# Output projection: the two halves of a token tile split to f16 in SBUF and turned by DMA instead of by TensorE

## The chip, the cores and the metric

The kernel runs on one core of a Trainium2 chip. The metric is the device time of one execution in microseconds (us), as the median of several runs.

## What is computed

One encoder layer over 4096 tokens plus 16 learned meta tokens, width 1024. A combined input projection feeds a Fourier branch (512 wide) and a grouped-query attention branch (8 query heads, 2 key/value heads of 64), both gated. Their outputs, side by side, go through one output projection, a residual add and a final RMSNorm:

```
u = rmsnorm(h, norm_g); proj = u @ w_in
f_out = fourier_branch(f_in) * silu(f_gate)            # 512 channels
a_out = attention_branch(q, k, v) * silu(a_gate)       # 512 channels
mixed = concat([f_out, a_out])                         # 1024 channels
h = h + mixed @ w_out
out = rmsnorm(h, final_g)[16:]
```

All inputs are float32. The kernel carries values as a sum of two f16 parts (a high part and what is left), so a product takes three matmuls: high x high, high x low, low x high.

## The kernel before

**Two phases.** `phase_a` does the input projection, the folding and the first half of the Fourier branch, and writes its results to DRAM. `phase_b` is attention. The Fourier branch's rest is dealt out among attention's first block; its result `f_out` lands in DRAM as `mf_d` (4096 x 512 f32). The order on every engine is the order in which the code is written; nothing reorders it.

**Pairs and steps.** `phase_b` runs over 32 pairs `i = 4b + p`: 8 blocks `b` of 512 queries, 4 pairs `p` of heads. A pair has 66 steps `j` (two heads, 33 key tiles each). Step `j`:

- `qk` (two matmuls of 512 columns, lines 1100 and 1101, into a PSUM tile `s`, of which there are two), then ACT's exp `pe` (line 1104), then the f16 rest `rr` (line 1106), on GpSimd (POOL) or, at the steps in `on_dve`, on VectorE;
- `pvm`, the product with the values (lines 1121 to 1128), of the step five before: `LAG = 5`. It reads `pe` and `rr`.

At the 16 steps in `AT` two score groups of the next pair are multiplied (line 1031, PSUM tile `m`, of which there are two) and reduced by VectorE (line 1033) to a row maximum.

**Output projection of the block before.** While pair `(b, p)` runs, the token tile `s = p` (128 tokens) of block `b-1` is projected. Steps of a pair that matter here: `TR = 12` (turn the tile), `O0 = 15` and `O1 = 39` (first matmul of the first and of the second half of the output columns; one matmul of 24 per step, line 1181, tile `po`), `NORM` (the final norm of the tile before). In a half, matmuls 0 to 11 read the Fourier channels and 12 to 23 the attention channels. So attention's part is first read at step 27.

Matmuls want the channels on the partitions, so the tile must be turned. `out_tr` does it at step 12: eight f32 transposes on TensorE (line 1164; four from `mf`, the Fourier half loaded from `mf_d`, four from `obs`, attention's output in SBUF) into one `m` tile, ACT's copy to the f16 high parts `mh` (line 1167) and at step 13 VectorE's subtraction to the low parts `ml` (line 1169).

**The tail.** The last block's four tiles are projected after attention's end. `tail_tr(s, part)` transposes four blocks into an `s` tile (line 1346; part 0 Fourier, part 1 attention), ACT writes the high parts (line 1349) and VectorE the low ones (line 1350) into `hv` and `lv`, which are the idle query buffers `qA` and `qB`; `tail_mm` multiplies (line 1361), `tail_end` normalises and stores.

**Queues.** Nearly all DMAs of `phase_b` are issued by SyncE (SP), which waits in order: gates `ag` (`gload`, line 802), queries of the next block (`qload`, lines 780 to 785; line 780 is a transposing DMA from DRAM), `mf` (line 1147), the residual `xr` (line 1152), the result `out` (line 1214).

Of the kernel before, what the change touches and what calls it, by code (L numbers as in the profile page):

```python
# [22 lines left out]
F32 = mybir.dt.float32  # L23
F16 = mybir.dt.float16
BF16 = mybir.dt.bfloat16
I32 = mybir.dt.int32
AF = mybir.ActivationFunctionType
ALU = mybir.AluOpType
# [4 lines left out]
P = 128  # L33
D = 1024
# [12 lines left out]
WS = 64.0  # L47
# [3 lines left out]
NQB = NTOK // QB  # L51
# [688 lines left out]
def phase_b(tc, a, pool, mm3, id32, id16, sc):  # L740
# [5 lines left out]
    V, S, T, G = nc.vector, nc.scalar, nc.tensor, nc.gpsimd  # L746
    dma, dma_t = nc.sync.dma_start, nc.sync.dma_start_transpose
    q_d, k_d, v_d, fg_d, ag_d, mf_d, wo_d, ld = (
        sc[n] for n in ("q_d", "k_d", "v_d", "fg_d", "ag_d", "mf_d", "wo_d", "ld"))
    LAG = 5  # L750
    with ExitStack() as st:
        bp = pool(st, "bp")
        w1 = pool(st, "b1", 1)
        w2 = pool(st, "b2", 2)
        wk = pool(st, "bw", LAG + 3)
        sm = pool(st, "bs", 2)
        pm = pool(st, "pm", 2, PSUM)
# [5 lines left out]
        qA = [bp.tile([P, NH, QB], F16, name=f"qA{i}") for i in range(2)]  # L763
        qB = [bp.tile([P, NH, QB], F16, name=f"qB{i}") for i in range(2)]
# [39 lines left out]


        wvh, wvl = ld["wv"]
        bias, stk8 = (w2.tile([P, 512], F32, tag="mf", name=n) for n in ("bias", "stk8"))
        stk = w1.tile([P, 4, P], F32, tag="hh", name="stk")
        thl = w1.tile([P, 2, 2, 4, P], F16, tag="yo", name="thl")
        mos = w2.tile([P, 4, 512], F32, tag="ob", name="mo")  # L810
# [329 lines left out]

            return qk, pvm

        pst = {}

        def load_mf(b, s):
            mf = w2.tile([P, 512], F32, tag="mf", name="mf")
            dma(mf, mf_d[b * QB + s * P:b * QB + s * P + P])
            pst[b, s] = [mf, None]

        def load_xr(b, s):  # L1150
            xr = pst[b, s][-1] = w2.tile([P, D], F32, tag="xr", name="xr")
            dma(xr, a["x"][b * QB + s * P:b * QB + s * P + P])

        def out_load(b, s):
            load_mf(b, s)
            load_xr(b, s)

        def out_tr(b, s):
            mf, xr = pst[b, s]
            t = pm.tile([P, 2, 512], F32, tag="m", name="m")  # L1160
            tv = t.rearrange("p a (b c)->p (a b) c", c=P)
            for j in range(8):
                src = mf[:, j * P:(j + 1) * P] if j < 4 else obs[b][:, s, (j - 4) * P:(j - 3) * P]
                T.transpose(tv[:, j], src, id32)  # L1164
            mh = ld["sh1"].tile([P, 8, P], F16, tag="mh", name="mh")
            ml = ld["sh1"].tile([P, 8, P], F16, tag="ml", name="ml")
            S.activation(mh, tv, AF.Copy)
            pst[b, s] = [mh, ml, xr]
            return lambda: V.tensor_tensor(out=ml, in0=tv, in1=mh, op=ALU.subtract)

        def out_units(b, s):

            d = {}

            def one(k, j):
                mh, ml, xr = pst[b, s]
                if j == 0:
                    d["po"] = pp.tile([P, 512], F32, tag="po", name="po")
                cs = slice(k * 512, (k + 1) * 512)
                i, w = j // 3, j % 3  # L1180
                T.matmul(d["po"], (ml if w == 2 else mh)[:, i],  # L1181
                         wol[i // 4][:, i % 4, cs] if w == 1 else woh[0][:, i, cs], start=j == 0, stop=j == 23)
                if j == 23:
                    if k == 0:
                        d["hh"] = w1.tile([P, D], F32, tag="hh", name="hh")
                    V.scalar_tensor_tensor(out=d["hh"][:, cs], in0=d["po"], scalar=1.0 / WS, in1=xr[:, cs],  # L1186
                                           op0=ALU.mult, op1=ALU.add)

            return [[(lambda k=k, j=j: one(k, j)) for j in range(24)] for k in range(2)], d

        def out_end(b, s, d):

            xr, hh = pst.pop((b, s))[-1], d["hh"]
            ss = sm.tile([P, 1], F32, tag="ss", name="ss")
            rf = sm.tile([P, 1], F32, tag="rf", name="rf")

            def square():
                S.activation(xr, hh, AF.Square, accum_out=ss)

            t = sm.tile([P, 1], F32, tag="r1t", name="r1t")  # L1200
            h = sm.tile([P, 1], F32, tag="r1h", name="r1h")

            def guess():
                V.tensor_scalar(out=ss, in0=ss, scalar1=1.0 / D, scalar2=EPS, op0=ALU.mult, op1=ALU.add)
                root0(rf, ss, t, h)

            def newton():
                root1(rf, t, h)

            def scale():  # L1210
                yo = w1.tile([P, D], F32, tag="yo", name="yo")
                V.scalar_tensor_tensor(out=yo, in0=hh, scalar=rf, in1=fgb[0], op0=ALU.mult, op1=ALU.mult)
                t0 = b * QB + s * P
                dma(a["out"][t0:t0 + P], yo)

            return square, guess, newton, newton, newton, scale
# [51 lines left out]
        def block0(g, mid):  # L1268
# [8 lines left out]
            if not flist and not fgb:  # L1277
# [3 lines left out]
                wo_load()  # L1281
                release()

        pend = []
        prev = None
        for i, (b, p) in enumerate(pairs):
            if p == 1 and b + 1 < NQB:
                qload(b + 1)
            if i > 4:
                out_load(b - 1, p)  # L1290
            elif i == 4:
                load_mf(0, 0)
            gs, last = [], {}
            if i + 1 < len(pairs):
                gs, meta, red, fin, put = max_units(i + 1)
                last = {61: red, 63: fin, 64: put}
                if meta:
                    last[MT] = meta[0]
            halves = None
            on_dve = {j + 2 for j in AT[:-1]} | {2 * NT + 1}  # L1300
            if i + 1 == len(pairs):
                on_dve = {j for j in range(2 * NT + 2) if j % 3}
            for j, (qk, pvm) in enumerate(stream(i)):
                qk(V if j in on_dve else G)
                if halves:
                    for k, o in ((0, O0), (1, O1)):
                        if o <= j < o + 24:
                            halves[0][k][j - o]()
                n = 2 if j in AT else 0
                if j == TR and b > 0:  # L1310
                    low = out_tr(b - 1, p)
                    halves = out_units(b - 1, p)
                for f in gs[:n]:
                    f()
                gs = gs[n:]
                if j in last:
                    last[j]()
                if i < 5:
                    block0(66 * i + j, j - 2 in AT)
                if i == 4 and j == 28:  # L1320
                    load_xr(0, 0)
                if j == LAG + 2 and i + 1 < len(pairs):
                    gload(i + 1)
                if j == 20 and i + 1 == len(pairs):
                    load_mf(b, 0)
                    load_mf(b, 1)
                    load_xr(b, 0)
                if j == TR + 1 and b > 0:
                    low()
                if j in NORM and prev:  # L1330
                    prev[NORM.index(j)]()
                if j == 62 and b > 0:
                    prev = out_end(b - 1, p, halves[1])
                pend.append(pvm)
                if len(pend) > LAG:
                    pend.pop(0)()


        b = NQB - 1
        hv, lv = (t[(b + 1) % 2].rearrange("p h (a c)->p (h a) c", c=P) for t in (qA, qB))  # L1340

        def tail_tr(s, part):
            src = pst[b, s][0] if part == 0 else obs[b][:, s]
            t = pq.tile([P, 512], F32, tag="s", name="s")
            for j in range(4):
                T.transpose(t[:, j * P:(j + 1) * P], src[:, j * P:(j + 1) * P], id32)
            x = slice(4 * (2 * s + part), 4 * (2 * s + part) + 4)
            tv = t.rearrange("p (j c)->p j c", c=P)
            S.activation(hv[:, x], tv, AF.Copy)
            V.tensor_tensor(out=lv[:, x], in0=tv, in1=hv[:, x], op=ALU.subtract)  # L1350
# [12 lines left out]
                                 start=i == 0 and w == 0, stop=i == 7 and w == 2, skip_group_check=True)  # L1363

        def tail_end(s):
            acc, xr = accs.pop(s), pst.pop((b, s))[1]
            yo = w1.tile([P, D], F32, tag="yo" if s % 2 else "hh", name="yo")
            ss = sm.tile([P, 2], F32, tag="ss2", name="ss2")
            rf = sm.tile([P, 1], F32, tag="rf", name="rf")
# [16 lines left out]
            t0 = b * QB + s * P  # L1386
            dma(a["out"][t0:t0 + P], yo)

        tail_tr(0, 0)
        tail_tr(1, 0)  # L1390
        prev[0]()
        while pend:
            pend.pop(0)()
# [2 lines left out]
        for f in prev[1:]:  # L1396
            f()
        load_xr(b, 1)
        tail_tr(0, 1)
        tail_tr(1, 1)  # L1400
        load_mf(b, 2)
        load_mf(b, 3)
        tail_mm(0, 1)
        tail_end(0)
        tail_tr(2, 0)
        tail_tr(2, 1)
        tail_mm(1, 1)
        tail_end(1)
        load_xr(b, 2)
        load_xr(b, 3)  # L1410
        tail_tr(3, 0)
        tail_tr(3, 1)
        tail_mm(2, 0)
        tail_mm(2, 1)
        tail_end(2)
# [138 lines left out]
```

## Time and profile before

| | |
|---|---|
| median of 3 runs | 3228.03 us (3224.39 to 3229.53) |
| the profiled execution | 3225.34 us, of which the span is 3223.6 us |
| busy: TensorE (PE), VectorE (DVE), ACT, POOL | 3169.3, 2366.2, 1671.4, 2270.3 us |
| granted TensorE clock | 0.995 |
| step 12 of pair 4, the first turned tile | 1123 us after the span's start |
| end of attention, start of the tail | about 3165 us |

Times in the profile are from the span's start. A row of a timeline has the start, the duration, the engine and what ran; `[0.19 <-PE s L1101]` at its end is how long the engine had been idle and what ended that. A row of the chain of waits has the start, the share of the end-to-end chain that the piece holds, and the piece. PE's matmuls overlap, so their duration is longer than their distance; the chain gives the distance.

### The profile page before, as it was taken

How to read it: one execution, taken by the hardware profiler on the slowest of the kernel's cores; microseconds unless marked ns; L12 is line 12 of the kernel's file. 1: busy time of each engine (PE TensorE's matmuls, PEld its weight loads, DVE VectorE, ACT ScalarE, POOL GpSimd, SP SyncE). 2: the span in 40 equal slices, each digit the busy share in tenths (PEclk: the TensorE clock that was granted, in tenths of full speed). 3: DMA queues.
4: the chain of work that ended last, by engine and by line, in shares of the span. 5: the costliest groups of instructions: out<-in, count | busy, mean ns of one | idle time of the engine just before them, and what ended most of it. 6: DMA issues, size and time to landing. Idle time of an engine off the chain costs nothing.

```text
span 3223.6 us, 77420 instructions
## 1 busy us (share of the span) xinstructions
PE 3169.3 (98%) x32531; PEld 1858.7 (58%) x32531; DVE 2366.2 (73%) x3213; ACT 1671.4 (52%) x2937; POOL 2270.3 (70%) x2174
## 2 busy tenths in 40 slices
PE   8999999998999999999999999999999999999998
PEld 4555555545666655555555555555555555555564
DVE  6666566647677777777787777778777877777764
ACT  5433333324555555555555555555555555555553
POOL 4655565537777777777777777777777777777762
PEclk9999999999999999999999999999999999999999
DMA  7444545548422300011001000100110010000011
GB/s 237 149 160 149 156 147 167 176 160 219 130 62 82 102 26 21 21 40 45 21 21 47 21 24 21 47 21 27 36 42 21 21 47 21 25 21 22 21 37 60
DMA packets 175344, 231.95 MB, mean 72 GB/s; under 512 B 71170, under 2 KB 119170, under 8 KB 172050
## 3 DMA queue, kind: packets, MB, share of 16 engines
q1 hardware_dynamic: 161170, 201.83, 20.5%
q10 hardware_dynamic: 13824, 25.17, 2.1%
q8 instruction: 254, 4.16, 0.5%
q14 instruction: 96, 0.79, 0.1%
HBM read 139.59 MB, written 66.38 MB: 64 GB/s over the span
## 4 chain that ended last, share of the span: by engine, by line
PE 74%; DVE 1%; issue 1%; ACT 0%; DMA 0%; POOL 0%; SPq 0%; ACTq 0%; DVEq 0%
PE s L1101 14%; PE s L1100 14%; PE o L1121 13%; PE po L1181 9%; PE m L1031 8%; PE o L1128 8%; PE o L1126 2%; PE o L1124 2%; PE pd L848 2%; PE m L1361 1%; PE m L1164 1%; DMA acs<-acs_d 0%; ACT pe L1104 0%; DVE thl L892 0%; DVE mx L1033 0%
## 5 line engine op out<-in xcount | busy, mean ns | idle before, releaser
L1106 POOL TENSOR_TENSOR rr<-pe 128x512 f16<-128x512 f32 x1572 | 1680.7, 1085 | 522.3 <-ACT pe L1104 516.3
L1104 ACT ACTIVATE pe<-s 128x512 f32<-128x512 f32 x2112 | 1260.7, 597 | 1030.3 <-PE s L1101 882.6
L1033 DVE TENSOR_REDUCE mx<-m 128x2 f32<-128x1024 f32 x1024 | 1206.3, 1220 | 181.8 <-PE m L1031 176.7
L1128 PE MATMUL o<-VV,rr 128*128 128x65 f16 x8448 | 975.5, 193 | 0.0
L1128 PEld LDWEIGHTS <-rr 128*128 128x128 f16 x8448 | 785.3, 98 | 168.3 <-POOL rr L1106 1.3
L1121 PE MATMUL o<-VV,pe 128*128 128x129 f16 x6336 | 840.5, 222 | 0.4 <-ACT tt L1132 0.4
L1101 PE MATMUL s<-qB,K 128*128 128x512 f16 x2112 | 800.8, 379 | 1.4 <-DVE qB L1068 1.4
L1100 PE MATMUL s<-qA,K 128*128 128x512 f16 x2112 | 800.0, 379 | 0.5 <-ACT pe L1104 0.5
L1121 PEld LDWEIGHTS <-pe 128*128 128x128 bf16 x6336 | 590.8, 97 | 361.7 <-issue 190.8
L1106 DVE TENSOR_TENSOR rr<-pe 128x512 f16<-128x512 f32 x540 | 450.7, 835 | 228.6 <-ACT pe L1104 224.4
L1124 PE MATMUL o<-VV,pe 128*128 128x65 f16 x2112 | 411.5, 195 | 0.0
L1126 PE MATMUL o<-VV,pe 128*128 128x64 f16 x2112 | 410.6, 194 | 0.0
L303 PE MATMUL ps<-wh,xh 128*128 128x512 f16 (+2 forms) x1032 | 353.7, 354 | 9.6 <-ACT xh L291 9.6
L304 PE MATMUL ps<-wl,xh 128*128 128x512 f16 (+2 forms) x1032 | 353.6, 354 | 2.3 <-DVE wl L274 2.3
L1031 PE MATMUL m<-K,qP 64*128 64x512 f16 x2048 | 314.1, 383 | 9.5 <-DMA qP<-qA 5.9
L306 PE MATMUL ps<-wh,xl 128*128 128x512 f16 x768 | 291.6, 380 | 0.0
L1126 PEld LDWEIGHTS <-pe 128*128 128x128 bf16 x2112 | 209.2, 99 | 0.0
L1124 PEld LDWEIGHTS <-pe 128*128 128x128 bf16 x2112 | 206.6, 98 | 0.0
L1101 PEld LDWEIGHTS <-K 128*128 128x128 f16 x2112 | 205.2, 97 | 1.6 <-issue 1.6
L1100 PEld LDWEIGHTS <-K 128*128 128x128 f16 x2112 | 203.6, 96 | 1.6 <-issue 1.4
L1031 PEld LDWEIGHTS <-qP 64*128 64x128 f16 x2048 | 59.8, 94 | 229.4 <-issue 221.5
L1181 PE MATMUL po<-woh,mh 128*128 128x512 f16 x448 | 169.8, 379 | 0.9 <-DVE hh L1186 0.9
(207 smaller groups left out, 3468.0 us busy)
## 6 DMA issues: line engine op xcount, KB each, us to landing
room<-x SPq DMA_DIRECT2D x32, 512.0 KB
xt<-xt SPq DMA_DIRECT2D x32, 512.0 KB
sg<-fx SPq DMA_DIRECT2D x16, 1024.0 KB
xr<-x SPq DMA_DIRECT2D x32, 512.0 KB
out<-yo SPq DMA_DIRECT2D x32, 512.0 KB
ct<-cdo SPq DMA_DIRECT2D x9, 1088.0 KB
fg_d<-g ACTq DMA_DIRECT2D x32, 256.0 KB
ag_d<-g ACTq DMA_DIRECT2D x32, 256.0 KB
```

The lines of the kernel that those rows point to most:

```text
L303: T.matmul(o, xh[:, d, :n], wh[:, d, c0:c1], start=d == 0, stop=False)
L1031: T.matmul(t[:, e], q[rs, p, s * P:(s + 1) * P], K[kv][rs, 0, c * 512:(c + 1) * 512], start=True, stop=True)
L1033: V.tensor_reduce(mx[:, s, :, c], t, axis=AX.X, op=ALU.max)
L1100: T.matmul(s, K[kv][:, 0, t * P:(t + 1) * P], qa, start=True, stop=False)
L1101: T.matmul(s, K[kv][:, 1, t * P:(t + 1) * P], qb, start=False, stop=True)
L1104: S.activation(pe, s, AF.Exp, scale=HD ** -0.5)
L1106: eng.tensor_tensor(out=rr, in0=pe, in1=hi, op=ALU.subtract)
L1121: T.matmul(o[:, c0:c0 + 129], hi[:, cs], va, start=t == 0 and s == 0, stop=t == NT, skip_group_check=True)
L1124: T.matmul(o[:, c0:c0 + 65], hi[:, cs], vh, start=False, stop=t == NT, skip_group_check=True)
L1126: T.matmul(o[:, c0:c0 + 64], hi[:, cs], vl, start=False, stop=t == NT, skip_group_check=True)
L1128: T.matmul(o[:, c0:c0 + 65], rr[:, cs], vh, start=False, stop=t == NT, skip_group_check=True)
L1181: T.matmul(d["po"], (ml if w == 2 else mh)[:, i], wol[i // 4][:, i % 4, cs] if w == 1 else woh[0][:, i, cs], start=j == 0, stop=j == 23)
```

## The change

The TensorE transposes of the output projection are replaced in the steady part, and for the Fourier half in the tail too. A half of a token tile (128 tokens x 512 channels, f32 in SBUF) is copied to f16 high parts by ACT and its low parts are subtracted by VectorE, both from SBUF to SBUF, side by side in one tile of 128 x 1024 f16. A transposing DMA from SBUF to SBUF turns the eight 128 x 128 blocks of it.

- Fourier half: `load_mf` at step 40 of the pair before, ACT at step 50, VectorE at 51, the DMA to `mt` at 53. For the first tile, in pair 4, the load stands at the pair's start and the steps are 6, 7 and 8.
- Attention half: ACT at step 12, VectorE and the DMA to `at` at step 13.
- Last pair: four Fourier tiles, loaded at steps 20, 31, 42, 53; ACT, VectorE and two DMAs (high parts to `hv`, low parts to `lv`) from steps 26, 37, 48 and 59.
- Tiles: `mf` shares a buffer with the new `ah` (tag `ml`), `hl` takes the tag `mh`, `mt` and `at` are new, one buffer each. The Fourier branch's `bias` and `stk8` share one buffer of tag `xr`.
- The tail transposes only attention's four blocks of each tile.

```diff
-        bias, stk8 = (w2.tile([P, 512], F32, tag="mf", name=n) for n in ("bias", "stk8"))
+        bs = w2.tile([P, 2, 512], F32, tag="xr", name="bs")
+        bias, stk8 = bs[:, 0], bs[:, 1]
...
         def load_mf(b, s):
-            mf = w2.tile([P, 512], F32, tag="mf", name="mf")
+            mf = mfs[b, s] = ld["sh1"].tile([P, 512], F32, tag="ml", name="mf")
             dma(mf, mf_d[b * QB + s * P:b * QB + s * P + P])
...
+        def mf_parts(b, s):
+            mf = mfs.pop((b, s))
+            hl = ld["sh1"].tile([P, 2, 512], F16, tag="mh", name="hl")
+            def high():
+                S.activation(hl[:, 0], mf, AF.Copy)
+            def low():
+                V.tensor_tensor(out=hl[:, 1], in0=mf, in1=hl[:, 0], op=ALU.subtract)
+            def turn():
+                mt = w1.tile([P, 8, P], F16, tag="mt", name="mt")
+                dma_t(mt, hl.rearrange("p w c->p (w c)"))
+                mts[b, s] = [mt]
+            def turn_last():
+                dma_t(hv[:, 8 * s:8 * s + 4], hl[:, 0])
+                dma_t(lv[:, 8 * s:8 * s + 4], hl[:, 1])
+            return high, low, turn_last if b + 1 == NQB else turn
...
         def out_tr(b, s):
-            mf, xr = pst[b, s]
-            t = pm.tile([P, 2, 512], F32, tag="m", name="m")
-            tv = t.rearrange("p a (b c)->p (a b) c", c=P)
-            for j in range(8):
-                src = mf[:, j * P:(j + 1) * P] if j < 4 else obs[b][:, s, (j - 4) * P:(j - 3) * P]
-                T.transpose(tv[:, j], src, id32)
-            mh = ld["sh1"].tile([P, 8, P], F16, tag="mh", name="mh")
-            ml = ld["sh1"].tile([P, 8, P], F16, tag="ml", name="ml")
-            S.activation(mh, tv, AF.Copy)
-            pst[b, s] = [mh, ml, xr]
-            return lambda: V.tensor_tensor(out=ml, in0=tv, in1=mh, op=ALU.subtract)
+            src = obs[b][:, s]
+            hl = ld["sh1"].tile([P, 2, 512], F16, tag="ml", name="ah")
+            S.activation(hl[:, 0], src, AF.Copy)
+            def low():
+                V.tensor_tensor(out=hl[:, 1], in0=src, in1=hl[:, 0], op=ALU.subtract)
+                at = w1.tile([P, 8, P], F16, tag="at", name="at")
+                dma_t(at, hl.rearrange("p w c->p (w c)"))
+                mts[b, s].append(at)
+            return low
...
-                T.matmul(d["po"], (ml if w == 2 else mh)[:, i],
+                T.matmul(d["po"], mts[b, s][i // 4][:, i % 4 + (4 if w == 2 else 0)],
...
+                if i == 4 and j == 6:
+                    ready = dict(zip((6, 7, 8), mf_parts(0, 0)))
+                if i + 1 == len(pairs):
+                    if 20 <= j < 60 and j % 11 == 9:
+                        load_mf(b, j // 11 - 1)
+                    if j >= 26 and j % 11 == 4:
+                        ready = dict(zip((j, j + 1, j + 2), mf_parts(b, j // 11 - 2)))
+                elif i >= 4:
+                    if j == 40:
+                        load_mf(*divmod(i - 3, 4))
+                    if j == 50:
+                        ready = dict(zip((50, 51, 53), mf_parts(*divmod(i - 3, 4))))
+                if j in ready:
+                    ready[j]()
...
-        tail_tr(0, 0)
-        tail_tr(1, 0)
         prev[0]()
...
-        tail_tr(2, 0)
-        tail_tr(2, 1)
+        tail_tr(2)
         tail_mm(1, 1)
         tail_end(1)
...
-        tail_tr(3, 0)
-        tail_tr(3, 1)
+        tail_tr(3)
```

**On TensorE** at step 12 of a steady pair, between the scores (lines 1100, 1101) and the product with the values (from line 1121), before:

```order
L1101 LDWEIGHTS K_7267
L1101 MATMUL s<-qB_7272,K_7267 128x512
L1164 MATMUL m<-id_72,mf 128x128 x4
L1164 MATMUL m<-id_72,ob 128x128 x4
L1121 LDWEIGHTS pe
L1121 MATMUL o<-VV,pe 128x129
```

The two rows of line 1164 stand there no more; the product with the values follows the scores directly, as at any other step. The matmuls of the output projection stay where they were and read `mt` and `at`.

**On ACT**, one pair from the end of one head to step 12, before (`tt` is the end of a head, `xr,ss` the square of the norm at step 9, `mh` step 12):

```order
L1132 ACTIVATE tt<-o 128x452
L1104 ACTIVATE pe<-s 128x512 x33
L1132 ACTIVATE tt<-o 128x452
L1104 ACTIVATE pe<-s 128x512 x5
L1198 ACTIVATE xr,ss<-hh 128x1024
L1104 ACTIVATE pe<-s 128x512 x3
L1167 ACTIVATE mh<-m 128x1024
```

and now (line numbers after the edit: 1105 is the exp, 1133 the end of a head, 1214 the square):

```order
L1133 ACTIVATE tt<-o 128x452
L1105 ACTIVATE pe<-s 128x512 x13
L1155 ACTIVATE hl<-mf 128x512
L1105 ACTIVATE pe<-s 128x512 x20
L1133 ACTIVATE tt<-o 128x452
L1105 ACTIVATE pe<-s 128x512 x5
L1214 ACTIVATE xr,ss<-hh 128x1024
L1105 ACTIVATE pe<-s 128x512 x3
L1178 ACTIVATE ah<-ob 128x512
```

One copy of 1024 elements out of PSUM at step 12 became two of 512 out of SBUF, one at step 50 of the pair before and one at step 12. VectorE's subtraction is split in the same way, to steps 51 and 13.

**On SP**, a pair in which the next block's queries are loaded, before:

```order
L1214 DMA out<-yo 128x1024
L780 DMA_TRANSPOSE qA_7269<-q_d 128x4x512 x2
L783 DMA qP_7273<-qA_7269 64x2x512 x4
L785 DMA qB_7271<-qA_7269 64x2048 x2
L1147 DMA mf<-mf_d 128x512
L1152 DMA xr<-x 128x1024
L802 DMA ag<-ag_d 128x4x128
L1214 DMA out<-yo 128x1024
```

and now (1230 is the result's store, 1148 the load of `mf`, 1173 the residual's):

```order
L1230 DMA out<-yo 128x1024
L1148 DMA mf<-mf_d 128x512
L1162 DMA_TRANSPOSE mt<-hl 128x8x128
L780 DMA_TRANSPOSE qA_7269<-q_d 128x4x512 x2
L783 DMA qP_7273<-qA_7269 64x2x512 x4
L785 DMA qB_7271<-qA_7269 64x2048 x2
L1173 DMA xr<-x 128x1024
L802 DMA ag<-ag_d 128x4x128
L1183 DMA_TRANSPOSE at<-ah 128x8x128
L1230 DMA out<-yo 128x1024
```

The `mt` DMA, which waits for VectorE's step 51, now stands ahead of the next pair's query loads and residual, and the `at` DMA between the gates and the store. In the whole program SP issues 64 more transposing DMAs: 28 to `mt`, 28 to `at`, 8 in the last pair.

More of the change, by code (lines that the diff above doesn't have):

```diff
@@ L1141, in step @@
             return qk, pvm
-        pst = {}
+        pst, mts, mfs = {}, {}, {}
         def load_mf(b, s):
-            mf = w2.tile([P, 512], F32, tag="mf", name="mf")
+            mf = mfs[b, s] = ld["sh1"].tile([P, 512], F32, tag="ml", name="mf")
             dma(mf, mf_d[b * QB + s * P:b * QB + s * P + P])
-            pst[b, s] = [mf, None]
+        def mf_parts(b, s):
[13 more added lines that the diff above has]
+            return high, low, turn_last if b + 1 == NQB else turn
@@ L1150, in load_xr @@
         def load_xr(b, s):
-            xr = pst[b, s][-1] = w2.tile([P, D], F32, tag="xr", name="xr")
+            xr = pst[b, s] = w2.tile([P, D], F32, tag="xr", name="xr")
             dma(xr, a["x"][b * QB + s * P:b * QB + s * P + P])
-        def out_load(b, s):
-            load_mf(b, s)
-            load_xr(b, s)
         def out_tr(b, s):
-            mf, xr = pst[b, s]
-            t = pm.tile([P, 2, 512], F32, tag="m", name="m")
-            tv = t.rearrange("p a (b c)->p (a b) c", c=P)
-            for j in range(8):
-                src = mf[:, j * P:(j + 1) * P] if j < 4 else obs[b][:, s, (j - 4) * P:(j - 3) * P]
-                T.transpose(tv[:, j], src, id32)
-            mh = ld["sh1"].tile([P, 8, P], F16, tag="mh", name="mh")
-            ml = ld["sh1"].tile([P, 8, P], F16, tag="ml", name="ml")
-            S.activation(mh, tv, AF.Copy)
-            pst[b, s] = [mh, ml, xr]
-            return lambda: V.tensor_tensor(out=ml, in0=tv, in1=mh, op=ALU.subtract)
+            src = obs[b][:, s]
@@ L1175, in one @@
             def one(k, j):
-                mh, ml, xr = pst[b, s]
                 if j == 0:
@@ L1185, in one @@
                         d["hh"] = w1.tile([P, D], F32, tag="hh", name="hh")
-                    V.scalar_tensor_tensor(out=d["hh"][:, cs], in0=d["po"], scalar=1.0 / WS, in1=xr[:, cs],
+                    V.scalar_tensor_tensor(out=d["hh"][:, cs], in0=d["po"], scalar=1.0 / WS, in1=pst[b, s][:, cs],
                                            op0=ALU.mult, op1=ALU.add)
@@ L1191, in out_end @@
         def out_end(b, s, d):
-            xr, hh = pst.pop((b, s))[-1], d["hh"]
+            xr, hh = pst.pop((b, s)), d["hh"]
             ss = sm.tile([P, 1], F32, tag="ss", name="ss")
@@ L1282, in block0 @@
                 release()
+        hv, lv = (t[NQB % 2].rearrange("p h (a c)->p (h a) c", c=P) for t in (qA, qB))
         pend = []
@@ L1289, in phase_b @@
             if i > 4:
-                out_load(b - 1, p)
+                load_xr(b - 1, p)
             elif i == 4:
                 load_mf(0, 0)
+            ready = {}
             gs, last = [], {}
@@ L1324, in phase_b @@
                 if j == 20 and i + 1 == len(pairs):
-                    load_mf(b, 0)
-                    load_mf(b, 1)
                     load_xr(b, 0)
@@ L1339, in phase_b, with tail_tr @@
         b = NQB - 1
-        hv, lv = (t[(b + 1) % 2].rearrange("p h (a c)->p (h a) c", c=P) for t in (qA, qB))
-        def tail_tr(s, part):
-            src = pst[b, s][0] if part == 0 else obs[b][:, s]
+        def tail_tr(s):
+            src = obs[b][:, s]
             t = pq.tile([P, 512], F32, tag="s", name="s")
@@ L1346, in tail_tr @@
                 T.transpose(t[:, j * P:(j + 1) * P], src[:, j * P:(j + 1) * P], id32)
-            x = slice(4 * (2 * s + part), 4 * (2 * s + part) + 4)
+            x = slice(8 * s + 4, 8 * s + 8)
             tv = t.rearrange("p (j c)->p j c", c=P)
@@ L1365, in tail_end @@
         def tail_end(s):
-            acc, xr = accs.pop(s), pst.pop((b, s))[1]
+            acc, xr = accs.pop(s), pst.pop((b, s))
             yo = w1.tile([P, D], F32, tag="yo" if s % 2 else "hh", name="yo")
@@ L1398, in phase_b @@
         load_xr(b, 1)
[L1399 to L1402, printed above, removed]
+        tail_tr(0)
+        tail_tr(1)
         tail_mm(0, 1)
         tail_end(0)
-        tail_tr(2, 0)
-        tail_tr(2, 1)
+        tail_tr(2)
         tail_mm(1, 1)
```

## The prediction

> **What bounds the kernel now.** I read the page's busy shares first, then the chain of waits, then the pair that holds a turned tile.
>
> ```profile
> span 3223.6 us, 77420 instructions
> PE 3169.3 (98%) x32531; PEld 1858.7 (58%) x32531; DVE 2366.2 (73%) x3213; ACT 1671.4 (52%) x2937; POOL 2270.3 (70%) x2174
> L1101 PE MATMUL s<-qB,K 128*128 128x512 f16 x2112 | 800.8, 379 | 1.4 <-DVE qB L1068 1.4
> L1100 PE MATMUL s<-qA,K 128*128 128x512 f16 x2112 | 800.0, 379 | 0.5 <-ACT pe L1104 0.5
> L1128 PEld LDWEIGHTS <-rr 128*128 128x128 f16 x8448 | 785.3, 98 | 168.3 <-POOL rr L1106 1.3
> ```
>
> PE is busy 98% of the span, and that alone proves little, since its matmuls overlap. The last columns say more: before the 4224 score matmuls PE stood idle 1.9 us in all, and its weight load waited 1.3 us for `rr`. So in attention nothing holds PE up, and what PE no longer does comes off the end, as long as nothing else becomes late. The chain around the turned tile of one pair shows what that is:
>
> ```profile
> 2669.23 0.22 PE s L1100
> 2669.45 0.22 PE s L1101
> 2669.67 0.06 PE o L1121
> ...
> 2670.23 0.22 PE s L1101
> 2670.45 0.87 PE m L1164 x8
> 2671.32 0.06 PE o L1121
> ```
>
> Step 11 goes from the scores straight to the product with the values; step 12 has 0.87 us of transposes between, on the chain and without a gap on either side.
>
> **Term 1: the steady transposes leave PE.** One such group per tile; ACT's copy that follows each counts the tiles:
>
> ```profile
> L1167 ACT ACTIVATE mh<-m 128x1024 f16<-128x1024 f32 x28 | 28.6, 1023 | 6.1 <-PE m L1164 6.1
> L1169 DVE TENSOR_TENSOR ml<-m,mh 128x1024 f16<-128x1024 f32 x28 | 34.3, 1225 | 30.7 <-ACT mh L1167 30.7
> ```
>
> 28 x 0.87 = 24.4 us, all of it on the path.
>
> **Term 2: the tail.** The chain, and PE's timeline at its three places:
>
> ```profile
> 3165.90 1.05 PE s L1346 x8
> ```
>
> ```profile
> 3185.70 0.60 PE L1346 MATMUL s<-id,mf 128*128 128x128 f32 x4
> 3186.14 0.60 PE L1346 MATMUL s<-id,ob 128*128 128x128 f32 x4
> 3186.57 0.38 PE L1361 MATMUL m<-woh,qA 128*128 128x512 f16 x1
> ...
> 3191.54 0.38 PE L1361 MATMUL m<-woh,qB 128*128 128x512 f16 x1
> 3192.64 0.66 PE L1346 MATMUL s<-id,mf 128*128 128x128 f32 x4 [0.72 <-DVE qB L1350]
> 3193.24 0.66 PE L1346 MATMUL s<-id,ob 128*128 128x128 f32 x4
> 3193.73 0.38 PE L1361 MATMUL m<-woh,qA 128*128 128x512 f16 x1
> ```
>
> The eight Fourier transposes at the tail's start go: 1.05 us. For tile 2, four of eight go: 0.87 us (3185.70 to 3186.57) become 0.44, so 0.43. For tile 3 PE is held from 3191.76 (the last matmul's start plus the 0.22 at which they follow each other) to 3193.73, 1.97 us, because four halves share two `s` tiles and the third waits until ACT and VectorE have emptied the first. With one `s` tile per token tile, tile 3 takes the one of tile 1, emptied long before, and needs 0.44 us: 1.53 saved. Sum 3.0 us. The end after the last matmul is unchanged.
>
> **Term 3: what takes the transposes' place.** Three things must be in time for it to cost nothing.
>
> *The attention half*, turned from step 13 and first read at step 27. When it can start: ACT's rows around step 12, and then in the chain the scores of step 14, the first output matmul of the tile (step 15) and its thirteenth (step 27).
>
> ```profile
> 2670.55 0.60 ACT L1104 ACTIVATE pe<-s 128x512 f32<-128x512 f32 x1 [0.19 <-POOL rr L1106]
> 2671.36 1.02 ACT L1167 ACTIVATE mh<-m 128x1024 f16<-128x1024 f32 x1 [0.21 <-PE m L1164]
> ```
>
> ```profile
> 2672.46 0.21 PE s L1100
> ...
> 2673.68 0.22 PE po L1181
> ...
> 2688.26 0.22 PE po L1181
> ```
>
> The new copy no longer waits for PE: it follows the exp at 2671.1. For 512 elements from SBUF I take the other copies and subtractions of that size, 0.63 us on ACT and 0.69 to 1.08 on VectorE:
>
> ```profile
> L378 ACT ACTIVATE qs<-t 128x512 f16<-128x512 f32 x32 | 20.0, 626 | 73.6 <-POOL t L363 73.6
> L379 DVE TENSOR_TENSOR qs<-t,qs 128x512 f16<-128x512 f32 x32 | 34.7, 1084 | 53.2 <-ACT qs L378 49.3 <-DMA sg<-fx 3.9
> ```
>
> ```profile
> 2670.39 0.69 DVE L1106 TENSOR_TENSOR rr<-pe 128x512 f16<-128x512 f32 x1 [0.22 <-ACT pe L1104]
> ```
>
> So SP can issue the DMA by 2671.1 + 0.63 + 1.08 = 2672.8. The thirteenth matmul, now 0.87 us earlier, comes at 2687.4: 14.6 us of cover. Before, no DMA turned anything out of SBUF. The nearest rows are the query loads, which turn 512 x 512 f16 out of DRAM, 512 KB against the 256 KB here; the load that needs the result starts the moment it has landed:
>
> ```profile
> 705.85 2.36 SPq L780 DMA_TRANSPOSE qA<-q_d  x1
> 711.21 1.35 SPq L783 DMA_DIRECT2D qP<-qA  x2
> ...
> 733.17 4.01 SPq L780 DMA_TRANSPOSE qA<-q_d  x1
> 740.72 1.28 SPq L783 DMA_DIRECT2D qP<-qA  x2
> ```
>
> 5.4 us on quiet queues, 7.6 us beside other loads. Half of the smaller (2.7 us, if it goes by bytes) and the larger whole are my ends; I take 5 us, nearer the row on quiet queues, since step 13 has little else on the DMAs. All of it lies within 14.6 us: 0.
>
> *The Fourier half* leaves at step 53 and is read at step 15 of the next pair, 28 steps later: 0. What it stands in front of on SP is the next pair's residual and, in one pair of four, the query loads; both are needed tens of steps later: 0. Only the first tile (pair 4) is close, since its DMA leaves at step 8:
>
> ```profile
> 1119.28 0.39 SPq L802 DMA_DIRECT2D ag<-ag_d  x1
> 1119.49 1.00 DVE L1106 TENSOR_TENSOR rr<-pe 128x512 f16<-128x512 f32 x1
> 1126.62 0.22 PE po L1181
> ```
>
> The subtraction follows the `rr` of step 7, which ends at 1120.5, so the DMA leaves at 1121.2 to 1121.6 and lands 2.7 to 7.6 us later, at 1123.9 to 1129.2; it is read at 1126.62 - 0.87 = 1125.75. That costs 0 to 3.4 us, once. With 5 us it is some 0.6 us.
>
> *ACT, VectorE, POOL.* ACT's 1.02 us at step 12 becomes 0.63 there and 0.63 at step 50; before its exps it idled 0.19 us even here, and an exp may start a step late, as `s` has two tiles: 0. VectorE's 1.23 becomes 0.69 to 1.08 twice (steps 13 and 51). POOL is where a loss could start, since it lags at the start of a pair:
>
> ```profile
> 2662.87 2.06 POOL L1106 TENSOR_TENSOR rr<-pe 128x512 f16<-128x512 f32 x2 [0.53 <-ACT pe L1104]
> 2664.89 0.52 POOL L1136 TENSOR_TENSOR ob<-tt 128x192 f32<-128x192 f32 x1
> ...
> 2667.00 13.42 POOL L1106 TENSOR_TENSOR rr<-pe 128x512 f16<-128x512 f32 x12
> 2680.74 1.04 POOL L1106 TENSOR_TENSOR rr<-pe 128x512 f16<-128x512 f32 x1 [0.32 <-ACT pe L1104]
> ```
>
> From 2662.87 it works without a pause for 17.6 us. The twelve (1.12 us each) are steps 5, 6, 8, 9, 10, 12 and on, since VectorE does 7 and 11. That of step 6 ends at 2669.24 and PE read it in step 11 at 2669.67, 0.43 us later and without a wait. That of step 9 ends at 2671.47; PE's step 14 (scores from 2672.46) reads it at 2672.89, and 0.87 us earlier from now on, at 2672.02: 0.55 us of cover, more than step 6 had. The transposes gave POOL a rest that it does not need: 0.
>
> **Sum.** 24.4 + 3.0 - 0.6 = 26.8 us. Against the profiled execution's 3225.34 us that is 3198.5; it lies 2.7 us below the median shown, 3228.03, from which I count: 3228.0 - 26.8 = 3201 us.
>
> A rule that speaks against the change: the Trainium skill ("VectorE: DVE Perf Modes", sections "The three transpose paths" and "Rules for kernel authors") gives 390 ns for turning a 128 x 128 bf16 block on TensorE and 1309 ns by DMA, and advises TensorE wherever the result may go to PSUM. This trace has 0.87 / 8 = 0.11 us a block on TensorE; for a DMA out of SBUF no run here shows it. If eight blocks came one behind the other, an estimate from that figure is 10.5 us, which the 14.6 us still cover; in pair 4 it would be late by 6 us, so by the rule the sum is 21 us and the time 3207 us.
>
> **Rivals.** *Slower: the attention half lands late.* If a transposing DMA out of SBUF is much dearer than one out of DRAM, PE stands at step 27 of every pair. Each us beyond 14.6 costs 28 us, and at 15.6 us the whole gain is gone. With four times the 5.4 us row, 21.4 us, it is 28 x 6.8 = 190 us: 3391 us. For it: no row shows the source in SBUF. Against it: it needs nearly three times what twice the bytes took.
>
> *Half: POOL's lag bites.* If VectorE's subtraction at step 13, which now reads SBUF as POOL does, holds POOL off for its whole length (1.0 us), step 10's `rr` and those behind it slip past their cover of 0.55 and PE waits 0.45 us a pair: 12.6 us back, 3214 us. For it: `rr` took VectorE 1.00 us at 1119.49 and 0.69 at 2670.39, so something shared can slow it. Against it: POOL's own `rr` takes 1.12 us in the stretch where VectorE works beside it and 1.04 at 2680.74, so POOL loses tenths, not its turn.
>
> *No change.* PE waits somewhere else for what it has gained, 3225 to 3231 us. The 1.9 us of waits before the scores speak against it: PE is ahead of nobody.
>
> *The blocks come one by one* (the slow end of the DMA's price in pair 4): 3207 us, faster still.
>
> **Chances.** My sum 0.77, the blocks one by one 0.05, POOL's lag 0.07, no change 0.03, late DMA 0.08. About 0.2% (6.5 us) is what a measurement of this kernel can tell from no change; the sum, the blocks and POOL's lag lie beyond it. Hence faster 0.89, same 0.03, slower 0.08. The range runs from 3195 (all three terms whole and the runs some us kinder, as the profiled one was) to 3214 (POOL's lag).
>
> **What would show it.** In the changed kernel's chain the 0.87 us pieces of line 1164 are gone and step 12 is as long as step 11, 0.78 us (2669.45 to 2670.23). A pair is 0.87 us shorter. PE's weight loads from `mt` and `at` show no wait for a DMA, but perhaps one in pair 4; if PE is idle before the thirteenth output matmul of each pair, the first rival is right. If the weight load of `rr` waits for POOL by more than a few us in all, it is the second. In the tail, the 0.72 us of idle time before tile 3's transposes are gone. The prediction is wrong if the time from the `at` DMA's issue to its first reader is not covered, or if a pair shortens by clearly less than 0.87 us with no DMA late.

## The result: 21 us faster, and the profile after

| | before | after |
|---|---|---|
| median (lowest to highest) | 3226.85 us (3224.39 to 3229.53, 4 runs) | 3205.68 us (3203.48 to 3206.03, 4 runs) |
| the profiled execution, its span | 3225.34, 3223.6 us | 3203.48, 3201.7 us |
| granted TensorE clock | 0.995 | 0.995 |

The ratio is 0.9933, 95% interval 0.9916 to 0.995: faster, by 0.5 to 0.84%. The medians lie 21.2 us apart and the profiled spans 21.9; the sum said 26.8, the forecast 3201. So the direction and the size are right, and some 5 us did not come. I look first for what was forecast, then for those 5 us.

The page of the changed kernel, first its busy times, then its costliest groups (the number after the last bar is the idle time before the group, then who ended it):

```profile
span 3201.7 us, 77151 instructions
PE 3146.1 (98%) x32291; PEld 1831.4 (57%) x32291; DVE 2373.2 (74%) x3241; ACT 1667.2 (52%) x2965; POOL 2304.3 (72%) x2174
L1101 PE MATMUL s<-qA,K 128*128 128x512 f16 x2112 | 799.6, 379 | 0.7 <-ACT pe L1105 0.7
L1102 PE MATMUL s<-qB,K 128*128 128x512 f16 x2112 | 800.3, 379 | 1.4 <-DVE qB L1069 1.4
L1129 PEld LDWEIGHTS <-rr 128*128 128x128 f16 x8448 | 784.5, 98 | 175.6 <-POOL rr L1107 7.4
```

PE is still busy for 98% of the span, and its score matmuls wait 2.1 us in all, next to nothing. One number is different in kind: the weight load of `rr` waits 7.4 us for POOL, where it waited 1.3. The chain of waits of the changed kernel, steps 12 and 14 of the pair that the prediction shows:

```profile
2656.11 0.21 PE s L1101
2656.33 0.22 PE s L1102
2656.54 0.06 PE o L1122
```

```profile
2657.69 0.21 PE s L1101
2657.90 0.22 PE s L1102
2658.12 0.06 PE o L1122
2658.17 0.17 PE o L1129
...
2658.40 0.03 PE o L1129
...
2658.61 0.22 PE s L1101
```

At step 12 the product with the values follows the scores at once; the 0.87 us of transposes are gone. But two steps later one matmul on `rr` holds 0.17 us of the chain, where the next of its line holds 0.03. From one score matmul to the next, step 14 takes 0.92 us (2657.69 to 2658.61) instead of 0.78: 0.14 us in this pair that were not there before. Of pairs 5 to 30, 19 have a step 14 that is 0.09 to 0.14 us longer than before, and 7 have not; together that is 2.5 us.

Where the time came from is read from three points of the chain: the first matmul of the first turned tile (1126.62 us before, shown with the prediction), the tail's first projecting matmuls, and the end. Of the kernel before:

```profile
3168.73 10.36 PE m L1361 x48
```

Of the changed kernel, with the last of the tail's transposes and what follows it:

```profile
1128.22 0.22 PE po L1197
...
3148.84 10.36 PE m L1389 x48
...
3171.59 0.44 PE s L1374 x4
3172.03 20.73 PE m L1389 x96
```

| us | before | after | gain | forecast |
|---|---|---|---|---|
| start to the first turned tile's matmul | 1126.62 | 1128.22 | -1.6 | 0.87 - 0.6 = 0.3 |
| from there to the tail's matmuls | 2042.11 | 2020.62 | 21.5 | 27 x 0.87 + 1.05 = 24.5 |
| from there to the end of the span | 54.87 | 52.86 | 2.0 | 0.43 + 1.53 = 2.0 |

The tail gave what was counted. The middle lacks 3.0 us, the start 1.9. Of the 3.0, step 14 accounts for 2.5; the other 0.5 is lost in the last pair, which the part on the prediction comes to.

### The profile page after: what moved, and what is told of

Its sections match the earlier page's. It is cut to its first block, busy times and chain, and to the rows that moved or that the text cites. A ratio compares the mean times of both kernels' runs of the same rounds, so it can differ in the third digit from the quotient of the medians.

```text
span 3201.7 us, 77151 instructions
## 1 busy us (share of the span) xinstructions
PE 3146.1 (98%) x32291; PEld 1831.4 (57%) x32291; DVE 2373.2 (74%) x3241; ACT 1667.2 (52%) x2965; POOL 2304.3 (72%) x2174
## 3 DMA queue, kind: packets, MB, share of 16 engines
q1 hardware_dynamic: 224658, 217.57, 23.6%
## 4 chain that ended last, share of the span: by engine, by line
PE 74%; DVE 1%; ACT 0%; DMA 0%; issue 0%; POOL 0%; SPq 0%; ACTq 0%; DVEq 0%; POOLq 0%
PE s L1102 14%; PE s L1101 14%; PE o L1122 13%; PE po L1197 9%; PE m L1032 8%; PE o L1129 8%; PE o L1127 2%; PE o L1125 2%; PE pd L849 2%; PE m L1389 1%; DMA acs<-acs_d 0%; ACT pe L1105 0%; POOL rr L1107 0%; DVE rr L1107 0%; DVE thl L893 0%
## 5 line engine op out<-in xcount | busy, mean ns | idle before, releaser
L1107 POOL TENSOR_TENSOR rr<-pe 128x512 f16<-128x512 f32 x1572 | 1709.9, 1105 | 469.9 <-ACT pe L1105 463.4
L1197 PE MATMUL po<-woh,mt 128*128 128x512 f16 x448 | 169.8, 379 | 1.0 <-DVE hh L1202 1.0
```

Source lines behind the costliest of these rows:

```text
L1107: eng.tensor_tensor(out=rr, in0=pe, in1=hi, op=ALU.subtract)
L1197: T.matmul(d["po"], mts[b, s][i // 4][:, i % 4 + (4 if w == 2 else 0)], wol[i // 4][:, i % 4, cs] if w == 1 else woh[0][:, i, cs], start=j ...
```

## The experiments

**The theories.** *A, POOL's lag:* the 0.14 us at step 14 are what the middle lacks; the `rr` of step 9, on POOL, ends just too late. *A1* says why: VectorE's own `rr` of step 11 runs beside it and holds it up. *C* is the rival: the new DMAs, by their traffic or by waits for them, take the 3 us. The other letters are told where the expectations name them. The time from the first output matmul to the tail, 2020.62 us above, is the yardstick in what follows, since it leaves out what differs by chance at the start.

**1. The changed kernel again**, as the base on the same chip.

> The changed kernel once more, beside the others on one chip. Its start of attention (first score matmul) was at 781.7 us after the span's start, 3.5 us later than in the kernel before, though nothing ahead of it was changed. Theory A (POOL's lag is what is missing of the gain; the start is chance): about 3205 us, the start of attention anywhere within 778 to 782. Theory B (the change itself delays the first phase): the start again near 781.7.

Measured: 3203.56 us (3201.88 to 3208.71, 5 runs) against 3227.19 for the kernel before (9 runs), ratio 0.9929 (0.9916 to 0.9941). Its chain:

```profile
1128.18 0.21 PE po L1197
...
3148.92 10.36 PE m L1389 x48
```

The stretch is 2020.74 us, the same as in the first profile to 0.1: the missing 3 us are there each time. Beside this base the kernel before is 23.6 us slower, against 21.2 in the first comparison. Theory B falls: attention starts at 780.3 us here, not near 781.7, at 778.9 and 778.1 in runs 2 and 3, and at 780.8 in run 7, which is the kernel before up to pair 4.

**2. One `rr` fewer on POOL.** Step 4's `rr` goes to VectorE in the pairs that turn a tile, so POOL is ahead when step 9 comes.

```diff
             on_dve = {j + 2 for j in AT[:-1]} | {2 * NT + 1}
+            if 4 <= i < len(pairs) - 1:
+                on_dve |= {4}
```

> The changed kernel, with the rest rr of step 4 on VectorE and not on POOL in pairs 4 to 30. Theory A (at step 14 PE waits 0.14 us for POOL's rr of step 9, in 27 to 28 pairs): POOL gets ahead by about 1 us, the wait goes, 3 to 4 us less than the changed kernel beside it, near 3202. Theory C (the missing part is the DMAs' traffic or their waits): no change.

Measured: 3199.71 us (3198.62 to 3200.92, 4 runs), ratio to the kernel before 0.9913 (0.99 to 0.9927); all its runs lie below all five of the changed kernel beside them. The group of the weight load, and the chain:

```profile
L1129 PEld LDWEIGHTS <-rr 128*128 128x128 f16 x8448 | 785.2, 98 | 171.4 <-POOL rr L1107 1.2
```

```profile
1125.88 0.26 PE po L1197
...
3143.95 10.36 PE m L1391 x48
```

The wait for POOL is back at 1.2 us, and the stretch is 2018.07 us: 2.55 of the missing 3.0 us came with it, and step 14 is as long as before in every pair. With this edit the kernel beats both given ones, and it is 27.5 us faster than the kernel before, where the sum said 26.8.

**3. VectorE leaves POOL alone.** The opposite edit: POOL gets one `rr` *more*, that of step 11, and VectorE no longer runs one beside step 9.

```diff
+            if 4 <= i < len(pairs) - 1:
+                on_dve -= {11}
```

> The changed kernel, with the rr of step 11 on POOL and not on VectorE in pairs 4 to 30. POOL has more to do, but VectorE's rr no longer runs beside POOL's rr of step 9, which took 1.55 us instead of 1.04. Theory A1 (what makes step 9 late is VectorE's SBUF operation beside it): rr of step 9 ends 0.5 us earlier, the wait at step 14 goes, 3 to 4 us less than the changed kernel. Theory A2 (POOL is simply short of time): the same or slower, by up to 28 x 0.5 = 14 us. Theory C: no change.

Measured: 3199.57 us (3197.49 to 3205.18, 4 runs), ratio to the kernel before 0.9916 (0.9902 to 0.9929). The wait and the chain:

```profile
L1129 PEld LDWEIGHTS <-rr 128*128 128x128 f16 x8448 | 785.3, 98 | 172.2 <-POOL rr L1107 1.9
```

```profile
1126.69 0.22 PE po L1197
...
3144.78 10.36 PE m L1391 x48
```

The stretch is 2018.09 us, as good as run 2, though POOL has more to do. The added `rr` stands behind that of step 9 and can't delay it, so this does not say that POOL's amount of work is without effect: run 2 took work away ahead of step 9 and won the same. It says that VectorE's `rr` beside POOL's is enough to cause the whole wait, as A1 has it, and that POOL's later `rr` have room for one more; A2 falls. The timelines show how: POOL's `rr` of steps 8 and 9 as one row of two (a row has start, duration, engine, line and operation), and VectorE beside it; first the kernel before, then the changed one, then this one.

```profile
2669.45 2.54 POOL L1106 TENSOR_TENSOR rr<-pe 128x512 f16<-128x512 f32 x2
```

```profile
2655.53 2.54 POOL L1107 TENSOR_TENSOR rr<-pe 128x512 f16<-128x512 f32 x2
2656.49 0.69 DVE L1107 TENSOR_TENSOR rr<-pe 128x512 f16<-128x512 f32 x1 [0.22 <-ACT pe L1105]
2657.79 0.83 DVE L1181 TENSOR_TENSOR ah<-ob,ah 128x512 f16<-128x512 f32 x1 [0.61 <-ACT ah L1178]
```

```profile
2652.16 2.04 POOL L1107 TENSOR_TENSOR rr<-pe 128x512 f16<-128x512 f32 x2
2654.41 1.33 DVE L1181 TENSOR_TENSOR ah<-ob,ah 128x512 f16<-128x512 f32 x1 [1.52 <-ACT ah L1178]
```

Two `rr` take 2.04 us alone and 2.54 beside VectorE's. In the changed kernel the second could have started at 2656.57 (1.04 after 2655.53), 0.08 after VectorE had begun; ending at 2658.07, it has lost 0.5 of VectorE's 0.69 us. And it goes the other way round: VectorE's subtraction takes 0.69 us when undisturbed (its shortest is 685 ns) and 1.33 here, where POOL was at work. Whoever comes second waits. The changed kernel itself shows both orders. In pair 27 POOL's `rr` of step 9 begins just ahead of VectorE's, so VectorE is the one that waits:

```profile
2801.07 2.03 POOL L1107 TENSOR_TENSOR rr<-pe 128x512 f16<-128x512 f32 x2
2802.09 1.57 DVE L1107 TENSOR_TENSOR rr<-pe 128x512 f16<-128x512 f32 x1 [0.23 <-ACT pe L1105]
```

POOL loses nothing there, and step 14 is not longer than before. So it is in all 7 pairs without the wait: POOL's `rr` keeps its 1.04 us and VectorE's takes 1.29 to 1.60. In the 19 others VectorE's keeps some 0.7 and POOL's takes 1.48 to 1.58. In most pairs the two begin within 0.05 us of each other.

The Trainium skill ("SBUF — State Buffer", section "Who interferes with whom") has this as a rule: a VectorE instruction with two SBUF inputs contends with a GpSimd instruction that reads SBUF, since both use one read port, and "it's an exclusive lock". The trace agrees, with the 0.5 us above and with pair 27.

**4. No transposing DMAs in the steady part.** The output matmuls of the steady pairs read one constant tile, and the 56 DMAs are not issued; ACT's copies and VectorE's subtractions stay. The values of the projection in blocks 0 to 6 are thereby left out.

```diff
+        fixed = w1.tile([P, 8, P], F16, tag="mt", name="fixed")
+        G.memset(fixed, 0.01)
...
-                mt = w1.tile([P, 8, P], F16, tag="mt", name="mt")
-                dma_t(mt, hl.rearrange("p w c->p (w c)"))
-                mts[b, s] = [mt]
+                mts[b, s] = [fixed]
...
-                at = w1.tile([P, 8, P], F16, tag="at", name="at")
-                dma_t(at, hl.rearrange("p w c->p (w c)"))
-                mts[b, s].append(at)
+                mts[b, s].append(fixed)
```

> The changed kernel without the 56 transposing DMAs of the steady part; the output matmuls of pairs 4 to 31 read one fixed tile, so the output projection's values are left out there, and all engine work stays. Theory A: the same time as the changed kernel (within 1 us), since no engine waited for them. Theory C (their traffic or their waits cost something): 2 to 5 us less.

Measured: 3205.72 us (3203.15 to 3206.29, 5 runs), against 3203.56 with the DMAs. The wait for POOL is still there:

```profile
L1129 PEld LDWEIGHTS <-rr 128*128 128x128 f16 x8448 | 784.6, 98 | 175.8 <-POOL rr L1107 6.9
```

The stretch from the first output matmul to the tail is 2020.85 us, against 2020.74 with the DMAs. Without the DMAs nothing is won, so neither their traffic nor a wait for them costs anything. C falls.

**5 and 6. How long is one of them?** In the changed kernel the transfer is wholly hidden, so its length can't be seen. Here the attention half is split and turned later, at steps 23 and 24 (`late = 11`), then at 25 and 26 (`late = 13`), each timed once, until PE has to wait at step 27.

```diff
+                late = 11 if i + 1 < len(pairs) else 0
...
-                    low = out_tr(b - 1, p)
+                if j == TR + late and b > 0:
+                    low = out_tr(b - 1, p)
...
-                if j == TR + 1 and b > 0:
+                if j == TR + 1 + late and b > 0:
```

> The changed kernel with the attention half's copy, subtraction and DMA eleven steps later (steps 23 and 24, in pairs 4 to 30), so that the DMA leaves about 1.3 us before its first reader at step 27 (14.9 us in the changed kernel). PE must then wait for what the DMA takes beyond 1.3 us, 27 times. If it takes 3 us (it left at 1124.09 in pair 4 and was read at 1127.8 without a wait): 27 x 1.7 = 46 us more, near 3250. If it takes the 5 us of the prediction: 100 us more, 3305. If the eight blocks come one behind the other at 1.31 us each (the rule weighed in the prediction): 250 us more, 3455.

> As before, but thirteen steps later (steps 25 and 26): the DMA leaves about 1.8 us after the time at which its first reader stood. A DMA of 3 us gives 27 x 4.8 = 130 us more than the changed kernel, near 3335; one of 5 us 184 us more; one of 10.5 us 330 us more. The difference between the two late kernels is the difference of their cover, whatever the DMA takes.

Measured: 3266.0 and 3414.66 us. The chain at one of the 27 waits, first at `late = 11`, then at 13, where the line names what the matmul waited for:

```profile
2722.65 3.07 DMA at<-ah
2725.72 0.05 issue
2725.76 0.39 PE po L1197
```

```profile
2599.34 3.09 DMA at<-ah
2602.43 0.05 issue
2602.48 0.61 PE po L1197
```

The DMA takes 3.1 us at both places. The waits of PE's matmuls in these two kernels (us, times, longest):

```profile
PE po L1197 <- DMA at<-ah: 51.3, 27, 2.7
```

```profile
PE po L1197 <- DMA at<-ah: 149.1, 27, 5.6
```

The losses against 3203.56 are 62 and 211 us, more than the 46 and 130 expected for a DMA of 3 us. PE itself stood for 51 and 149 us: 1.9 us each time (2.7 once), and 5.5. What lies beyond that is the clock, above all at `late = 13`, where the first matmul after the wait holds 0.61 us of the chain instead of 0.39. Two stretches of that kernel, the end of the wait and the 2.6 us after it (length, busy time and instructions of PE, PEld, DVE, ACT and POOL, then the granted clock, the DMAs' share and GB/s):

```profile
2599.00:2602.40 3.40, 0.00 (x0) 0.00 (x0) 0.28 (x1) 0.00 (x0) 0.00 (x0) 0.95 0.40 77
2602.40:2605.00 2.60, 2.52 (x16) 1.43 (x17) 0.00 (x0) 0.31 (x1) 0.00 (x0) 0.50 0.02 6
```

And after two of the shorter waits of `late = 11`, in pair 25 and in pair 6:

```profile
2725.70:2728.00 2.30, 2.23 (x26) 1.41 (x27) 0.34 (x1) 0.62 (x2) 0.00 (x0) 1.00 0.03 7
```

```profile
1294.20:1296.20 2.00, 1.98 (x13) 1.15 (x14) 0.00 (x0) 0.00 (x0) 0.00 (x0) 0.50 0.00 0
```

After each of the long waits the clock is at 0.50, here for some 3 us and for up to 6 in other pairs; a pair loses 1.4 to 2.9 us beyond PE's idle time, 59 in all. After 23 of the short waits it stays up and the pair loses 0.17 us beyond the idle time. After the other 4 (pairs 6, 18, 19 and 22) it falls to 0.50 as well, and the pair loses 1.7 to 1.8. With PE's idle time that makes 208 and 62 us over the 27 pairs, nearly all of the 211 and the whole of the 62.

**7. The control: the kernel before with run 2's edit.** If step 4's `rr` on VectorE were simply a better order, it would help there too.

```diff
             on_dve = {j + 2 for j in AT[:-1]} | {2 * NT + 1}
+            if 4 <= i < len(pairs) - 1:
+                on_dve |= {4}
```

> The kernel before with the rr of step 4 on VectorE in pairs 4 to 30, the edit that took 4 us from the changed kernel. Theory A (the edit removes a wait that the change made): here PE waited 1.3 us in all for rr, so no change, within 1 us of 3227. Theory D (the edit is worth 4 us by itself, whatever the transposes do): 3223.

Measured: 3228.71 us (3223.07 to 3231.41, 11 runs) against 3227.31 (15 runs), ratio 0.9999 (0.999 to 1.0008): no change, and theory D falls. Its stretch from the first output matmul to the tail is 2042.11 us, that of the kernel before to 0.01. So POOL's lag cost nothing before, and after the change the same edit is worth 4 us by the medians and 2.6 in the stretch. It is the transposes' going that uncovered it.

## Why the prediction was right, and where its sum was off

**The steady transposes (24.4 us) and the tail (3.0).** Right. Step 12 of the chain is as long as any other; the tail gave 2.0 us and its 1.05 us at attention's end stand in the middle stretch, which with run 2 comes to 2042.11 - 2018.07 = 24.0 of the 24.5.

**"ACT, VectorE, POOL: 0".** This is the step that failed, by 3.4 us: 2.5 at step 14, 0.4 in pair 4 and 0.5 in the last pair. First step 14. The cover of POOL's `rr` at step 9 was put at 0.55 us, by the row "13.42 ... x12" as 1.12 us each. That mean hid two kinds: `rr` of 1.04 us and some of 1.5, where VectorE runs beside it, and step 9 is one of the slow ones. In the row of two shown above the kernel before ends it at 2669.45 + 2.54 = 2671.99, not at 2671.47. Read at 2672.89, its cover was 0.90 us, and 0.87 of that went with the transposes. What is left, 0.03, is less than the weight load that stands between (98 ns), and PE waits up to 0.14 us in 19 pairs. "The transposes gave POOL a rest that it does not need" was wrong: it needed just that rest.

Then the last pair. ACT's copies (0.62 us each) cost nothing in the steady pairs, as said, but in the last one a copy of a Fourier half, at step 37, stands ahead of the end of a head and of the exp of step 38. ACT's rows there, before and after (the scores of that step begin at 3137.04 and at 3117.69):

```profile
3137.24 0.55 ACT L1132 ACTIVATE tt<-o 128x452 f32<-128x452 f32 x1
3137.73 0.60 ACT L1104 ACTIVATE pe<-s 128x512 f32<-128x512 f32 x1
```

```profile
3117.81 0.62 ACT L1155 ACTIVATE hl<-mf 128x512 f16<-128x512 f32 x1
3118.33 0.54 ACT L1133 ACTIVATE tt<-o 128x452 f32<-128x452 f32 x1
3118.76 0.60 ACT L1105 ACTIVATE pe<-s 128x512 f32<-128x512 f32 x1
```

The exp follows its scores 1.07 us later instead of 0.69. The chain goes on from it through VectorE's `rr` and the addition that frees `po` to PE, and steps 38 and 39 take 0.50 us longer than before. Run 2 has the same 0.50, and it is what its stretch still lacks.

**The rival of POOL's lag** named the right engine and the wrong neighbour. It laid it to the new subtraction at step 13; the runs show the `rr` of step 11, which stood there before the change. The subtraction does hold POOL up as the rival had it (POOL's `rr` of step 10 takes 1.48 us, from 2658.04), but PE does not wait for that one; only in pair 4 does it wait for what the new subtraction delays (see the first tile below). The rival's price, 0.45 us a pair, was three times what came. By the signs that the prediction names, this rival showed itself: the wait for `rr` is 7.4 us in all, and most pairs shorten by 0.73 us, not 0.87. And what I held against it, that POOL "loses tenths, not its turn", was wrong: it does lose its turn, for what is left of VectorE's instruction.

**The attention half, 5 us by estimate, covered by 14.6.** Covered, and cheaper. In the changed kernel SP issues it here, and the thirteenth output matmul comes 14.9 us later; the two rows are of SP's timeline and of the chain:

```profile
2658.69 1.27 SPq L1183 DMA_TRANSPOSE at<-ah  x1
```

```profile
2673.62 0.22 PE po L1197
```

The transfer takes 3.1 us at the two places shown (runs 5 and 6), near the low end of 2.7 to 7.6, the one that went by bytes. So the rival of the late half had nearly five times the time that it needed. The rival of the blocks one by one falls too: eight blocks in 3.07 us are 0.38 us each, where the 1309 ns of the Trainium skill ("VectorE: DVE Perf Modes", "The three transpose paths") would have made 10.5 by estimate.

**The first tile, 0.6 us.** The DMA cost nothing, but POOL did. The rows of VectorE's subtraction for the Fourier half (shortest, median, longest in ns), of the `mt` DMA, and the chain at that place:

```profile
L1158 DVE TENSOR_TENSOR hl<-mf,hl x32: 682/684/1522, 1122.5 to 3142.4; 128x512 f16<-128x512 f32 x32
L1162 SPq DMA_TRANSPOSE mt<-hl x28: 1237/1239/2079, 1124.1 to 3068.1; - x28
```

```profile
1122.01 2.90 POOL rr L1107 x2
1124.91 0.05 issue
1124.96 0.20 PE o L1129
```

The DMA leaves at 1124.1 and, with 3.1 us, has landed at 1127.2, before 1128.22. VectorE's 1.52 us is the longest of the 32, and POOL's two `rr` beside it take 2.90 us and end the chain's wait; the kernel before needs 2.49 for the same two. Step 11 of this pair is 0.41 us longer than before, and in run 2 it is not. So a cost near the forecast's 0.6 was there, but that is luck: it came from the neighbours and not from the DMA.

**What is left of the gap.** The start is 1.9 us worse than forecast in the profiled execution. Pair 4 itself does a little better than forecast there (a gain of 0.47 us for 0.3); it begins 2.06 us late. In the chain the first score matmul of that pair stands at 1111.59 in the kernel before and at 1113.65 in the changed one, but at 1114.59 in run 7, whose code is that of the kernel before up to this place. The runs with the changed kernel's code up to there have it between 1111.72 and 1115.22 (runs 1, 2, 3, 5 and 6). So 2 us lie within what differs from one execution to the next. That makes up the 4.9 us between the sum and the profiled spans: 2.5 from POOL at step 14, 0.5 from ACT in the last pair, 2.1 of spread at the start, less 0.2 in pair 4.

## What to carry to other kernels

When work leaves the bounding engine, everything that was covered by it comes earlier by that much: look up, for each engine that feeds it, the single instruction with the least cover around that place, and never take its end from the mean of a merged row. If the lag lies in two engines' use of SBUF at the same moment, taking away the instruction beside it is worth as much as taking work off the slow engine: run 3 gave POOL more to do and was 4 us faster. Look at the last round of a loop by itself, where work that is spread elsewhere comes together. The transposing DMA out of SBUF, with 14.9 us to land, was free on this kernel, which TensorE bounds.

## What I had not expected of the hardware

- POOL's subtraction of 512 columns takes 1.04 us alone and about 1.5 with VectorE's beside it; VectorE's takes 0.69 alone and up to 1.6 where POOL came first. It is a wait for one's turn, not a general slowing: in each pair one of the two is slow and the other is not.
- The transposing DMA from SBUF to SBUF turns eight blocks of 128 x 128 f16 in 3.07 us, less than the 5.4 us of the query load out of DRAM with twice the bytes.
- PE's clock fell to 0.50 after each of the 27 waits in which PE stood for 5.5 us, and after 4 of the 27 in which it stood for 1.9 to 2.7. The Trainium skill ("TensorE: Matmul & The Clock Gate", section "Part 1: The HAM clock gate") has the clock fall after at least one idle window of about 3.4 us; the long waits agree with that, but three of the four falls came after 1.9 us of standing, so here a shorter time was enough.
